# Row-norm Newton steps on VectorE, earlier row loads and re-used buffers for the last gate products in a streaming encoder layer

## Chip, cores, metric

One NeuronCore of a Trainium2 chip runs the whole kernel. The metric is the device time of one execution in microseconds (us). TensorE (PE in the profile) multiplies, VectorE (DVE) and GpSimd (POOL) do elementwise work, ScalarE (ACT) does activations and copies, SyncE (SP) only starts transfers.

## What is computed

One layer of a chunk-causal encoder over 2048 prompt rows and 64 sample rows of width 1024, in float32, with two head groups that share one input product:

```python
h = rms_norm(x, norm_mix_g); z = h @ w_in              # [c_q 384 | c_kv 256 | k_rope 32 | GLU 1024]
q = rms_norm(c_q) @ w_uq;  k, v = expand(rms_norm(c_kv) @ w_ukv, rope(k_r))
attn = softmax(q k^T * scale, chunk-causal) @ v         # 8 heads
u = g[..., :512] * sigmoid(g[..., 512:])                # the gate product
conv = silu(layer_norm(causal_depthwise_conv(u, 31 taps)))
x += concat(rms_norm(attn), rms_norm(conv)) @ w_out
x += square(relu(rms_norm(x) @ w_ff_up)) @ w_ff_down
x += sigmoid(rms_norm(x) @ w_gate) * (p @ w_proj)
y = rms_norm(x, norm_final_g)
```

Every `rms_norm` needs 1/sqrt(mean square) of each row.

## The kernel before

The 17 row tiles (16 of 128 rows and one of 64) form three blocks of two pieces, `T0` and `T1`, of two or three tiles. Each matrix operand is split into a high and a low part, so every product is three matmuls (`mm3`, lines 180 to 182).

**Phase 1** goes through the blocks: latents (`rows`, `latents`, `q_latents`), key and value expansion, queries, and four gate products per piece (`glu(T, j, w)` with j from 0 to 3). A gate product fills two PSUM banks, ScalarE takes the sigmoid of one into a tile `sg` (line 396; two buffers), VectorE multiplies it by the other (397), and SP writes it to memory as `u_s` (398). In the last block PSUM leaves only two banks for these products, so the next one can't begin before line 396 has read the last. For piece `T1` of the last block two slices of the tile are also transposed by TensorE (`new_conv`, 582). Near the end of blocks 0 and 1 the next block's rows are loaded (`load_h`, 236), normalised (`scaled`, 200) and transposed into `thi` and `tlo` (`operand`, 212 to 215). The tile `h` that takes a row tile has four buffers of 4 KB per partition, given out in turn; `queries` also takes one per piece for its table of cosines and sines. The convolution of earlier pieces (`conv_steps`, 614) runs on VectorE as a background sequence: `pin` lets some of its steps follow given instructions.

**The row norms**: `sumsq` squares and sums on ScalarE (162); `rstd` (145 to 157) takes the sums of up to three tiles (up to three columns), makes v (147) and a first guess by integer arithmetic (148, 150) on VectorE, and then does three Newton steps of four instructions each on GpSimd (153 to 156). Layer norms in `conv_steps` call the same function with `tag` "c"; all others with an empty tag.

**Phase 2** is attention. Its pools are laid over phase 1's memory: the first, `ka`, holds the keys and values of the first of three rotating heads (`k0h`, `k0l`, `v0`) and begins where phase 1's pool `p` begins, whose first tile is `h`. So `k0h` (9.25 KB per partition) covers two of the four buffers of `h` and part of the third, and `k0l` the rest of the third and the fourth. Each loads when what lay there is done with: GpSimd starts two transfers into each (lines 668 and 679) and then those into `v0`. TensorE first takes row maxima of scores (719), then products of queries and keys, then those with the values (763, 764). `issue_after` ties the first 24 steps of the maxima to the sigmoid of the gate product j=2 of the last piece. **Phase 3** is the output product, the feed-forward layer, the gate, and the final norm with the write of y (954 to 956).

The order of the instructions on each engine is made by a planner: it takes what is ready by its own reckoning, earlier lines of the program first. Each engine then runs its queue strictly in that order.

Of the kernel before, what the change touches and what calls it, by code (L numbers as in the profile page):

```python
# [9 lines left out]
F32 = mybir.dt.float32  # L10
# [4 lines left out]
ALU = mybir.AluOpType  # L15
# [4 lines left out]
P = 128  # L20
D = 1024
# [46 lines left out]
class Body:  # L68
# [72 lines left out]
    def rstd(self, ss, n, d, eps, tag=""):  # L141
        nc = self.nc
        v = self.sp.tile([P, 4], F32, name=tag + "rv")
        y = self.sp.tile([P, 4], F32, name=tag + "ry")
        t = self.sp.tile([P, 4], F32, name=tag + "rt")
        v, y, t = v[:, :n], y[:, :n], t[:, :n]
        nc.vector.tensor_scalar(out=v, in0=ss, scalar1=1.0 / d, scalar2=eps, op0=ALU.mult, op1=ALU.add)
        nc.vector.tensor_scalar(out=t.bitcast(I32), in0=v.bitcast(I32), scalar1=1, scalar2=None,
                                op0=ALU.logical_shift_right)
        nc.vector.tensor_scalar(out=y.bitcast(I32), in0=t.bitcast(I32), scalar1=-1, scalar2=0x5F3759DF,  # L150
                                op0=ALU.mult, op1=ALU.add)
        for _ in range(3):
            nc.gpsimd.tensor_tensor(out=t, in0=y, in1=y, op=ALU.mult)  # L153
            nc.gpsimd.tensor_tensor(out=t, in0=t, in1=v, op=ALU.mult)
            nc.gpsimd.tensor_scalar(out=t, in0=t, scalar1=-0.5, scalar2=1.5, op0=ALU.mult, op1=ALU.add)
            nc.gpsimd.tensor_tensor(out=y, in0=y, in1=t, op=ALU.mult)  # L156
        return y

    def sumsq(self, out, x, w):
# [63 lines left out]
    def phase1(self):  # L223
        nc, tc, I, O = self.nc, self.tc, self.I, self.O
        self.banks((0, 1, 2, 7), (4, 5, 6), 3)
        with ExitStack() as c:
            p = c.enter_context(tc.tile_pool(name="p1", bufs=2))
            pw = c.enter_context(tc.tile_pool(name="p1w", bufs=2))

            nw = 7  # L230
            def load_h(piece):
                hs = []
                for t in piece.tiles:
                    r0, n = TILES[t]
                    h = p.tile([P, D], F32, name="h", bufs=4)
                    nc.sync.dma_start(out=h[:n, :], in_=I["x"][r0:r0 + n, :])
                    hs.append(h)
                return hs

            def early_t(piece, hs, i):  # L240

                T = make_t(piece, hs)
                y = self.sp.tile([P, 4], F32, name="y0", bufs=2)
                nc.gpsimd.tensor_copy(out=y[:, :3], in_=self.norms(hs, piece.tiles))
                d = self.vp.tile([P, 30 + 384], F32, name="cu", bufs=2)
                for j in range(3):
                    nc.vector.tensor_scalar(out=d[:, j * P:(j + 1) * P], in0=self.ident, scalar1=y[:, j:j + 1],
                                            scalar2=None, op0=ALU.mult)
                tr = self.tr()
                nc.tensor.matmul(tr[:, :384], wide[0][:, 384:], d[:, :384], start=True, stop=True)  # L250
                nc.scalar.copy(out=wide[i][:, :384], in_=tr[:, :384])
                return (*T, y, wide[i][:, :384])
# [7 lines left out]
            def weights(parts, k, c):  # L260

                out = []
                step = WC // c
                for a in range(0, k, step):
                    b = min(k, a + step)
                    x = []
                    raw = pw.tile([P, WC], F32, name="raw")
                    hi = pw.tile([P, WC], F32R, name="whi", bufs=nw)
                    lo = pw.tile([P, WC], F32R, name="wlo", bufs=nw)
                    r, hi, lo = (x[:, :(b - a) * c].rearrange("p (k c) -> p k c", c=c) for x in (raw, hi, lo))  # L270
                    nc.sync.dma_start(out=r, in_=parts[:, a:b, :])
                    self.split(r, hi, lo)
                    out += [(hi[:, i, :], lo[:, i, :]) for i in range(b - a)]
                return out
# [102 lines left out]

                return make

            def glu(T, j, w, n=3):  # L380

                piece, th, tl = T[:3]
                pi = self.pieces.index(piece)
                N = piece.n
                pa, pb = self.mm(), self.mm()
                for ps, c in ((pb, slice(P, 2 * P)), (pa, slice(0, P))):
                    for k in range(KD):
                        self.mm3(ps[:, :N], w[k][0][:, c], w[k][1][:, c], th[:, k, :N], tl[:, k, :N],
                                 k == 0, k == KD - 1)
                u = pw.tile([P, 384], F32, name="sg")  # L390
                if len(T) > 3:
                    nc.vector.tensor_tensor(out=u, in0=pb[:, :N], in1=T[4], op=ALU.mult)
                    nc.scalar.activation(out=u, in_=u, func=AF.Sigmoid)
                    nc.vector.tensor_tensor(out=u, in0=u, in1=T[4], op=ALU.mult)
                else:
                    self.sig[piece, j] = nc.scalar.activation(out=u[:, :N], in_=pb[:, :N], func=AF.Sigmoid)
                r = nc.vector.tensor_tensor(out=u[:, :N], in0=pa[:, :N], in1=u[:, :N], op=ALU.mult)
                nc.sync.dma_start(out=self.u_s[pi][j], in_=u[:, :N])
                if pi == len(self.pieces) - 1:
                    self.new_conv(pw, u, j)  # L400
                self.pin(r, n)

            hs = load_h(self.pieces[0])
# [5 lines left out]
            T0 = early_t(self.pieces[0], hs, 0)  # L409
# [4 lines left out]
            hs = load_h(self.pieces[1])  # L414
            T1 = early_t(self.pieces[1], hs, 1)
            for bi, block in enumerate(self.blocks):
                kv0, cols0 = latents(T0, wkv)
                cq0 = q_latents(T0, wcq)
                kv1, cols1 = latents(T1, wkv)
                if bi == 0:  # L420
                    cq1 = q_latents(T1, wcq)
                wukv = weights(I["wukv"], 2, 1024)
                if bi == 0:
                    past = self.past_keys(p)
                    g0 = weights(I["wglu"][0], KD, 256)
                    q0 = queries(T0, cq0)
                    self.expand_k(p, *past, wukv)
                    glu(T0, 0, g0)
                    self.expand_v(p, *past, wukv)
                    k0 = keys(T0, kv0)  # L430
                    wuq = weights(I["wuq"], 3, 768)
                    glu(T1, 0, g0)
                else:
                    k0 = keys(T0, kv0)
                    q0 = queries(T0, cq0)
                    cq1 = q_latents(T1, wcq)
                    wuq = weights(I["wuq"], 3, 768)
                    g0 = weights(I["wglu"][0], KD, 256)
                self.expand(p, cols0, *k0, wukv)
                k1 = keys(T1, kv1)  # L440
                q0(wuq)
                q1 = queries(T1, cq1)
                if bi:
                    glu(T0, 0, g0)
                self.expand(p, cols1, *k1, wukv)
                g1 = weights(I["wglu"][1], KD, 256)
                q1(wuq)
                if bi:
                    glu(T1, 0, g0)
                g2 = weights(I["wglu"][2], KD, 256)  # L450
                if bi == 2:
                    self.banks((0, 1), (4, 5, 6), 3)
                glu(T0, 1, g1)
                if bi == 0:
                    self.bg = chain(self.conv_steps(0), self.conv_steps(1))
                g3 = weights(I["wglu"][3], KD, 256)
                glu(T1, 1, g1)
                if bi < 2:
                    n0, n1 = self.blocks[bi + 1]
                    wkv = weights(I["wkv"], KD, KVL + ROPE)  # L460
                    hs = load_h(n0)
                    self.scaled(hs, n0, hs)
                glu(T0, 2, g2)
                glu(T0, 3, g3)
                if bi < 2:
                    T0 = make_t(n0, hs)
                    hs = load_h(n1)
                    self.scaled(hs, n1, hs)
                glu(T1, 2, g2, 1)
                glu(T1, 3, g3, 1)  # L470
                if bi < 2:
                    wcq = weights(I["wcq"], KD, QL)
                    T1 = make_t(n1, hs)
# [772 lines left out]
```

## Time and profile before

| what | value |
|---|---|
| median of 3 runs | 3009.92 us (3006.69 to 3010.46) |
| the profiled execution | 3011.01 us, its span 3009.2 us |
| TensorE busy | 2912.3 us, 97% of the span |
| VectorE / ScalarE / GpSimd busy | 65% / 41% / 26% |
| mean granted TensorE clock | 0.990 of full speed |

The span runs from the first to the last instruction; the profiled execution's time is 1.8 us longer. An engine's idle time counts only where TensorE, or the end of the kernel, waits for it.

### The profile page before, as it was taken

The page shows a single profiled execution, that of the slowest core. Times are in us where ns is not written, and L with a number is a line of the kernel's source. Part 1 is how long each engine was busy: PE and PEld are TensorE (multiplying, and loading weights), DVE is VectorE, ACT ScalarE, POOL GpSimd, SP SyncE. Part 2 cuts the span into 40 slices and gives each one's busy share as a digit, 9 for nine tenths or more (in the row PEclk, how much of TensorE's full clock was granted, in tenths as well). Part 3 has the DMA queues.
Part 4 walks back from the last instruction along what each step waited for, and adds up shares of the span by engine and source line. Part 5 has one row for each costly group of instructions (what it writes and reads, how often), then busy time and mean ns, then how long its engine had stood idle before and what let it go on. Part 6 is the DMA issues. An engine that isn't in the chain of part 4 may idle for free.

```text
span 3009.2 us, 42569 instructions
## 1 busy us (share of the span) xinstructions
PE 2912.3 (97%) x15666; PEld 2568.8 (85%) x15666; DVE 1957.0 (65%) x3592; ACT 1242.5 (41%) x2388; POOL 782.1 (26%) x1526
## 2 busy tenths in 40 slices
PE   8998998899999899999999999999999999999998
PEld 7998898677777689999998889988988799999986
DVE  4489694888888756776665457868865544444463
ACT  6334343778878742223224343223234422221242
POOL 3021523878887610003002120012022200000001
PEclk9999999999999999999999999999999999999999
DMA  6636258633231221222112241222223412211131
GB/s 203 208 101 206 84 182 162 104 73 57 59 57 42 83 97 45 80 79 76 61 59 84 85 168 63 98 65 84 97 79 95 140 49 81 88 57 57 64 94 46
DMA packets 148601, 279.13 MB, mean 93 GB/s; under 512 B 38136, under 2 KB 78824, under 8 KB 146952
## 3 DMA queue, kind: packets, MB, share of 16 engines
q1 hardware_dynamic: 123800, 244.35, 25.5%
q0 software_dynamic: 24592, 32.06, 5.6%
q8 instruction: 123, 2.02, 0.3%
q14 instruction: 86, 0.70, 0.1%
HBM read 225.67 MB, written 51.28 MB: 92 GB/s over the span
## 4 chain that ended last, share of the span: by engine, by line
PE 78%; DVE 9%; POOL 4%; issue 4%; DMA 3%; ACT 2%; SPq 0%; DVEq 0%; ACTq 0%; POOLq 0%
PE mm L180 24%; PE mm L181 23%; PE mm L182 23%; PE tr L212 2%; PE low L764 2%; PE acc L763 2%; DVE mx L720 2%; DVE cacc L614 1%; DVE pl L756 1%; PE tr L719 1%; DMA u_s<-sg 1%; DVE ql L706 1%; POOL rt L153 1%; ACT ph L754 1%; POOL ry L156 0%
## 5 line engine op out<-in xcount | busy, mean ns | idle before, releaser
L181 PE MATMUL mm<-tlo,uh 128*128 128x384 f32 (+2 forms) x1488 | 481.4, 324 | 0.0
L180 PE MATMUL mm<-thi,uh 128*128 128x384 f32 (+2 forms) x1488 | 481.1, 324 | 0.0
L182 PE MATMUL mm<-thi,ul 128*128 128x384 f32 (+2 forms) x1488 | 480.9, 323 | 0.0
L614 DVE SCALAR_TENSOR_TENSOR cacc<-cu,cw,cacc 128x384 f32<-128x384 f32 (+2 forms) x720 | 414.3, 590 | 6.7
L1005 ACT ACTIVATE rl<-mm 128x384 f32<-128x384 f32 (+1 forms) x192 | 88.3, 460 | 644.9 <-PE mm L182 644.4
L180 PE MATMUL mm<-wdh,ah 128*128 128x512 f32 x896 | 349.2, 391 | 2.2 <-DVE x L1082 1.7
L181 PE MATMUL mm<-wdl,ah 128*128 128x512 f32 x896 | 348.4, 390 | 0.0
L182 PE MATMUL mm<-wdh,al 128*128 128x512 f32 x896 | 345.0, 390 | 0.0
L760 POOL TENSOR_TENSOR rs<-rs,ph 128x512 f32<-128x512 f32 (+5 forms) x304 | 326.4, 1077 | 40.3 <-ACT ph L754 25.9
L1082 DVE SCALAR_TENSOR_TENSOR x<-mm,y,x 128x512 f32<-128x512 f32 x224 | 166.3, 748 | 212.0 <-PE mm L182 210.1
L153 POOL TENSOR_TENSOR rt<-ry 128x3 f32<-128x3 f32 (+2 forms) x150 | 40.3, 269 | 987.3 <-DVE ry L150 979.4
L181 PEld LDWEIGHTS mm<-tlo,uh 128*128 128x128 f32 x1488 | 280.2, 188 | 0.6
L180 PEld LDWEIGHTS mm<-thi,uh 128*128 128x128 f32 x1488 | 279.9, 188 | 0.7
L182 PEld LDWEIGHTS mm<-thi,ul 128*128 128x128 f32 x1488 | 280.1, 188 | 0.1
L166 DVE TENSOR_TENSOR wdl<-raw,wdh 128x1024 fp32r<-128x1024 f32 x139 | 170.5, 1228 | 112.1 <-ACT wdh L165 110.9
L756 DVE TENSOR_TENSOR pl<-mm,ph 128x512 fp32r<-128x512 f32 (+5 forms) x344 | 193.9, 575 | 43.3 <-ACT mm L755 30.2
L754 ACT ACTIVATE ph<-mm 128x512 fp32r<-128x512 f32 (+5 forms) x344 | 175.9, 511 | 86.8 <-PE mm L182 59.0
L165 ACT CAST wdh<-raw 128x1024 fp32r<-128x1024 f32 x139 | 145.8, 1050 | 158.6 <-DMA raw<-in_wdn 91.8
L180 PEld LDWEIGHTS mm<-wdh,ah 128*128 128x128 f32 x896 | 168.3, 188 | 37.6 <-DVE x L1082 2.2
L182 PEld LDWEIGHTS mm<-wdh,al 128*128 128x128 f32 x896 | 168.2, 188 | 35.0
L181 PEld LDWEIGHTS mm<-wdl,ah 128*128 128x128 f32 x896 | 168.3, 188 | 33.8
L166 DVE TENSOR_TENSOR ul<-raw,uh 128x1024 fp32r<-128x1024 f32 x104 | 128.7, 1237 | 99.7 <-ACT uh L165 98.9
(309 smaller groups left out, 6682.5 us busy)
## 6 DMA issues: line engine op xcount, KB each, us to landing
raw<-in_wup SPq DMA_DIRECT2D x96, 512.0 KB, 3.3
raw<-in_wdn SPq DMA_DIRECT2D x96, 512.0 KB, 3.3
raw<-in_wglu SPq DMA_DIRECT2D x24, 512.0 KB, 4.7
raw<-in_wout SPq DMA_DIRECT2D x24, 512.0 KB, 4.7
raw<-in_wgate SPq DMA_DIRECT2D x24, 512.0 KB, 3.9
v_s<-vst SPq DMA_DIRECT2D x36, 256.0 KB, 2.8
v<-v_s POOLq DMA_DIRECT2D x8, 1152.0 KB, 7.9
h<-in_x SPq DMA_DIRECT2D x16, 512.0 KB, 4.4
```

The costliest lines, as they stand in the source:

```text
L153: nc.gpsimd.tensor_tensor(out=t, in0=y, in1=y, op=ALU.mult)
L165: self.nc.scalar.copy(out=hi, in_=raw)
L166: return (eng or self.nc.vector).tensor_tensor(out=lo, in0=raw, in1=hi.bitcast(F32), op=ALU.subtract)
L180: t.matmul(ps, sh, mh, start=start, stop=False)
L181: t.matmul(ps, sh, ml, start=False, stop=False)
L182: t.matmul(ps, sl, mh, start=False, stop=stop)
L614: nc.vector.scalar_tensor_tensor(out=a, in0=U[:, k:k + W], scalar=w, in1=a, op0=ALU.mult, op1=ALU.add)
L754: nc.scalar.activation(out=ph[b:, s], in_=ps[b:, s], func=AF.Exp)
L756: nc.vector.tensor_tensor(out=pl[b:, s], in0=ps[b:, s], in1=ph[b:, s].bitcast(F32), op=ALU.subtract)
L760: nc.gpsimd.tensor_tensor(out=rs[b:, s], in0=rs[b:, s], in1=ph[b:, s].bitcast(F32), op=ALU.add)
L1005: nc.scalar.activation(out=rl[:, :N], in_=ps[:, :N], func=AF.Relu)
L1082: r = nc.vector.scalar_tensor_tensor(out=x1[t][:n, cs], in0=ps[:n, :], scalar=Y[q][:n, j:j + 1], in1=x1[t][:n, cs], op0=ALU.mult, op1=ALU.add)
```

## The change

Three edits. In `rstd`, calls without a tag do each Newton step with three instructions on VectorE instead of four on GpSimd; calls with tag "c" stay. In blocks 0 and 1 the loads of the next block's first piece stand two gate products (and two weight loads) earlier in the program; their normalisation stays where it was. In the last block the gate products j=2 and j=3 of both pieces write into tiles `h` instead of `sg`.

```diff
         for _ in range(3):
-            nc.gpsimd.tensor_tensor(out=t, in0=y, in1=y, op=ALU.mult)
-            nc.gpsimd.tensor_tensor(out=t, in0=t, in1=v, op=ALU.mult)
-            nc.gpsimd.tensor_scalar(out=t, in0=t, scalar1=-0.5, scalar2=1.5, op0=ALU.mult, op1=ALU.add)
-            nc.gpsimd.tensor_tensor(out=y, in0=y, in1=t, op=ALU.mult)
+            if tag:
...
+            else:
+                nc.vector.scalar_tensor_tensor(out=t, in0=y, scalar=-0.5, in1=y, op0=ALU.mult, op1=ALU.mult)
+                nc.vector.tensor_tensor(out=t, in0=t, in1=v, op=ALU.mult)
+                nc.vector.scalar_tensor_tensor(out=y, in0=t, scalar=1.5, in1=y, op0=ALU.add, op1=ALU.mult)
...
-            def glu(T, j, w, n=3):
+            def glu(T, j, w, n=3, last=False):
...
-                u = pw.tile([P, 384], F32, name="sg")
+                u = p.tile([P, D], F32, name="h", bufs=4)[:, :384] if last else pw.tile([P, 384], F32, name="sg")
...
                 if bi:
                     glu(T1, 0, g0)
+                if bi < 2:
+                    n0, n1 = self.blocks[bi + 1]
+                    hs = load_h(n0)
                 g2 = weights(I["wglu"][2], KD, 256)
...
                 glu(T1, 1, g1)
                 if bi < 2:
-                    n0, n1 = self.blocks[bi + 1]
                     wkv = weights(I["wkv"], KD, KVL + ROPE)
-                    hs = load_h(n0)
                     self.scaled(hs, n0, hs)
-                glu(T0, 2, g2)
-                glu(T0, 3, g3)
+                glu(T0, 2, g2, last=bi == 2)
+                glu(T0, 3, g3, last=bi == 2)
...
-                glu(T1, 2, g2, 1)
-                glu(T1, 3, g3, 1)
+                glu(T1, 2, g2, 1, bi == 2)
+                glu(T1, 3, g3, 1, bi == 2)
```

## Rows read from the trace of the kernel before

**Rows 1.** The page's part 1: busy us, share of the span, instructions.
```profile
PE 2912.3 (97%) x15666; PEld 2568.8 (85%) x15666; DVE 1957.0 (65%) x3592; ACT 1242.5 (41%) x2388; POOL 782.1 (26%) x1526
```

**Rows 2.** Windows: length; busy us of PE, PEld, DVE, ACT, POOL; clock; DMA.
```profile
225.00:300.00 75.00, 65.36 (x404) 62.18 (x404) 68.52 (x138) 32.19 (x67) 14.26 (x43) 0.95 0.64 204
...
352.00:367.00 15.00, 8.52 (x42) 7.05 (x43) 11.52 (x17) 4.88 (x12) 12.09 (x30) 0.81 0.12 44
361.50:374.00 12.50, 9.93 (x37) 8.22 (x38) 11.99 (x23) 3.85 (x9) 4.43 (x7) 0.50 0.12 45
...
471.50:477.00 5.50, 5.50 (x18) 5.31 (x19) 0.96 (x2) 0.59 (x1) 0.00 (x0) 0.50 1.83 297
507.00:515.00 8.00, 4.31 (x14) 2.62 (x15) 5.89 (x24) 3.26 (x6) 4.32 (x9) 0.78 0.67 164
```

**Rows 3.** Waits of PE from 467 to 476 us: total, times, longest.
```profile
PE mm L180 <- ACT sg L396: 4.3, 1, 4.3
```

**Rows 4.** VectorE's timeline at the end: start, duration, instruction [idle before, releaser].
```profile
3000.21 0.15 DVE L148 TENSOR_SCALAR rt<-rv 128x1 int32<-128x1 int32 x1
3000.40 0.15 DVE L150 TENSOR_SCALAR ry<-rt 128x1 int32<-128x1 int32 x1
3003.87 1.28 DVE L954 SCALAR_TENSOR_TENSOR x<-x,ry,gfin 64x1024 f32<-64x1024 f32 x1 [3.32 <-POOL ry L156]
```

**Rows 5.** Tile ry: duration ns minimum/median/maximum, first and last start, forms.
```profile
L153 POOL TENSOR_TENSOR rt<-ry x150: 184/195/2161, 9.5 to 3002.8; 128x3 f32<-128x3 f32 x117, 128x2 f32<-128x2 f32 x24, 128x1 f32<-128x1 f32 x9
...
L150 DVE TENSOR_SCALAR ry<-rt x50: 148/169/1145, 9.3 to 3000.4; 128x3 int32<-128x3 int32 x39, 128x2 int32<-128x2 int32 x8, 128x1 int32<-128x1 int32 x3
```

**Rows 6.** VectorE's timeline in block 1 and at its end.
```profile
262.95 0.55 DVE L570 TENSOR_TENSOR q<-cq,h 128x384 f32<-128x384 f32 x1
...
273.66 0.16 DVE L150 TENSOR_SCALAR ry<-rt 128x3 int32<-128x3 int32 x1
273.73 0.74 DVE L535 TENSOR_TENSOR ktl<-mm,kth 128x256 fp32r<-128x256 f32 x2
...
351.60 2.07 DVE L200 TENSOR_SCALAR h<-h,ry 128x1024 f32<-128x1024 f32 x3 [2.70 <-POOL ry L156]
...
359.79 3.31 DVE L306 SCALAR_TENSOR_TENSOR kv<-kv,ry,gkv 128x256 f32<-128x256 f32 x3 [3.48 <-POOL ry L156]
```

**Rows 7.** GpSimd's timeline between blocks 1 and 2.
```profile
354.21 2.16 POOL L153 TENSOR_TENSOR rt<-ry 128x3 f32<-128x3 f32 x1
...
358.82 0.22 POOL L638 TENSOR_SCALAR nb<-nb 128x1 f32<-128x1 f32 x1
```

**Rows 8.** ScalarE's timeline, at two waits of phase 1.
```profile
359.08 0.81 ACT L639 ACTIVATE cs<-cs,nb,cry 128x512 f32<-128x512 f32 x1 [10.32 <-POOL nb L638]
...
470.85 0.44 ACT L396 ACTIVATE sg<-mm 128x320 f32<-128x320 f32 x1 [8.88 <-DMA u_s<-sg]
```

**Rows 9.** GpSimd's timeline: transfers into the first key tile.
```profile
453.86 0.57 POOL L668 DMA_DIRECT2D k0h<-kr_sh  x1 [42.10 <-DMA q_s<-cq]
...
455.07 0.53 POOL L679 DMA_DIRECT2D k0h<-k_s0h  x1
```

**Rows 10.** SP's timeline: a row load of block 2, and the last gate tile's write.
```profile
263.52 0.34 SPq L236 DMA_DIRECT2D h<-in_x  x1
...
507.24 0.34 SPq L398 DMA_DIRECT2D u_s<-sg  x1
```

**Rows 11.** Tile u_s, 497 to 512 us: writes of gate tiles, issue to landing.
```profile
DMA to landing us min/median/max: 2.1/2.1/2.2
```

**Rows 12.** Tile k0h, 450 to 520 us: its two transfers, issue to landing.
```profile
DMA to landing us min/median/max: 6.9/9.2/11.5
```

**Rows 13.** TensorE's timeline: first maxima and first score product of phase 2.
```profile
506.52 0.28 PE L719 MATMUL tr<-k0h,qh 128*128 128x256 f32 x1
...
515.01 0.63 PE L180 MATMUL mm<-qh,k0h 128*128 128x512 f32 x1
```

**Rows 14.** VectorE's timeline late in phase 2.
```profile
1003.37 1.02 DVE L147 TENSOR_SCALAR rv<-ss 128x3 f32<-128x3 f32 x1 [0.90 <-ACT junk L162]
```

More of the change, by code (lines that the diff above doesn't have):

```diff
@@ L152, in rstd @@
         for _ in range(3):
-            nc.gpsimd.tensor_tensor(out=t, in0=y, in1=y, op=ALU.mult)
-            nc.gpsimd.tensor_tensor(out=t, in0=t, in1=v, op=ALU.mult)
-            nc.gpsimd.tensor_scalar(out=t, in0=t, scalar1=-0.5, scalar2=1.5, op0=ALU.mult, op1=ALU.add)
-            nc.gpsimd.tensor_tensor(out=y, in0=y, in1=t, op=ALU.mult)
+            if tag:
+                nc.gpsimd.tensor_tensor(out=t, in0=y, in1=y, op=ALU.mult)
+                nc.gpsimd.tensor_tensor(out=t, in0=t, in1=v, op=ALU.mult)
+                nc.gpsimd.tensor_scalar(out=t, in0=t, scalar1=-0.5, scalar2=1.5, op0=ALU.mult, op1=ALU.add)
+                nc.gpsimd.tensor_tensor(out=y, in0=y, in1=t, op=ALU.mult)
+            else:
+                nc.vector.scalar_tensor_tensor(out=t, in0=y, scalar=-0.5, in1=y, op0=ALU.mult, op1=ALU.mult)
+                nc.vector.tensor_tensor(out=t, in0=t, in1=v, op=ALU.mult)
+                nc.vector.scalar_tensor_tensor(out=y, in0=t, scalar=1.5, in1=y, op0=ALU.add, op1=ALU.mult)
         return y
```

## The prediction, made before the change was run

> **What bounds the kernel now.** I read the page's busy line first, then windows, then the timelines around each hole of TensorE. TensorE is busy for 2912.3 of 3009.2 us [rows 1], so the change can only win in the 97 us in which it is idle, in stretches where it runs at half its granted clock, and in the tail behind its last matmul. The reader should see three places. Between blocks 1 and 2 TensorE worked 8.52 of 15 us, and then ran at a granted clock of 0.50 (its 1.2 GHz level) while busy for 9.93 us [rows 2]: 6.5 us idle and about half of 9.93, 5.0 us, lost to the clock. Before the last gate products it waited 4.3 us [rows 3] and ran 5.50 busy us at 0.50 behind it [rows 2], another 2.75. And at the very end VectorE waits 3.32 us for GpSimd [rows 4].
>
> **Newton steps: the cost of one norm.** There are 50 norms without the tag (150 instructions of line 153, three a norm) [rows 5]. Each loses 12 GpSimd instructions (0.195 us by the median of line 153) and gains 9 on VectorE. The trace of before has no such instruction on VectorE; the nearest rows are the small integer ones of lines 148 and 150 beside them: 0.15 to 0.17 us each, started 0.19 us apart where one needs the other [rows 4, 5], and only 0.07 us ahead of an instruction that doesn't need them [rows 6]. So a norm costs VectorE between 9 x 0.07 = 0.6 and 9 x 0.19 = 1.7 us.
>
> **The tail.** Line 150 starts at 3000.40 and line 954 at 3003.87 [rows 4]. With nine steps of 0.19 us behind line 150, line 954 starts at about 3000.40 + 10 x 0.19 = 3002.3: 1.6 us gained. Nothing else runs there, so I take it whole.
>
> **Between blocks 1 and 2.** GpSimd runs the untagged chains mixed with the layer norm's chain. One multiply of three numbers took 2.16 us, and the layer norm's last step (line 638) was done only at 359.0 [rows 7]. ScalarE had stood behind it for 10.32 us [rows 8], with the copies that feed TensorE queued after it; VectorE waited 2.70 and 3.48 us for the two untagged chains [rows 6]. Without the untagged steps GpSimd has only the layer norm left. The full prize is 6.5 + 5.0 = 11.5 us, the least is nothing, if the convolution steps that VectorE mixes in hold the nine steps back as long as GpSimd did. VectorE has idle time to fit them in (the two waits), so I take three quarters: 8.6 us gained.
>
> The Trainium skill, page "SBUF — State Buffer", section "Who interferes with whom", says that a VectorE instruction with two SBUF inputs and a GpSimd instruction that reads SBUF exclude each other for a whole instruction. The 2.16 us multiply agrees: it overlapped VectorE's work. By that rule the Newton steps on VectorE, all with two SBUF inputs, can now be the ones that block; where that would matter is a rival below.
>
> **VectorE's extra load.** In 225 to 300 us VectorE is busy 68.52 of 75 us and TensorE idle almost 10 [rows 2]. Three norms fall there and some four in the like stretch of block 2. Seven norms at 0.6 to 1.7 us are 4 to 12 us of VectorE time. At best the 6.5 us left free in that window hide them (0), at worst all of it delays TensorE (12). VectorE already ends waits there, so I take 3 us lost. Elsewhere (phase 3, the gate products) VectorE has room and TensorE none to give: nothing.
>
> **Row loads moved.** Per block these are two or three transfers on SP's queue, put ahead of the loads of two gate weights, of the next latents' weights and of two writes of gate tiles. But a load can't start before its buffer of `h` is free: the third one of block 2 started at 263.52, right behind the last VectorE instruction that reads the table in that buffer (262.95 plus 0.55) [rows 6, 10]. That reader doesn't move, and the load ran far ahead of its place in the program already. I cost it at 0; with the cover gone, one transfer on the queue ahead of a weight is its issue time of 0.34 us [rows 10], times six. On the other side, earlier loads gain nothing that a held buffer allows.
>
> **Gate tiles in `h`: what it removes.** At 453.86 GpSimd starts loading the first head's keys [rows 9]. These transfers crowd the write of an earlier gate tile: ScalarE stood 8.88 us for it [rows 8], and TensorE 4.3 [rows 3]. But the stalled product is j=1, which the change leaves in `sg`. It is relieved all the same, since the key loads no longer run at that time (next paragraph). Gain: 4.3 + 2.75 = 7.0 us.
>
> **What it adds.** The four tiles take the four buffers of `h` in turn, and the last of them (piece T1, j=3) gets the third buffer, which `k0h` and `k0l` share. Before, the key load waited for the last reader of `h`, at 453 us. Now it waits until the very last gate tile is written out. That write was issued at 507.24 [rows 10], 0.7 us behind the last gate matmul, and lands 2.1 us later [rows 11]; GpSimd can then issue, some 3.0 us behind the last matmul. `k0h` is complete when its second transfer lands: 455.07 + 11.5 - 453.86 = 12.7 us after the first issue [rows 9, 12]. Phase 2's first maxima came at 506.52, at once behind the gate products [rows 13]; now they come 15.7 us behind. TensorE has nothing else to do. Behind the waiting transfers in GpSimd's queue stand those for the second head and the layer norm's steps; they are not due at once. What comes back: in 507 to 515 TensorE was idle for 3.7 us [rows 2], on work of VectorE and ScalarE that can now be done during the wait; I take back 3.0. Cost 12.7 us, between 9 (faster landing without other traffic) and 18 (values late too).
>
> **The sum.** -1.6 - 8.6 + 3 + 0 - 7.0 + 12.7 = -1.5 us against the profiled execution's 3011.0, which is 1.1 above the median. I forecast 3008 us: no change that can be told. About 0.2%, 6 us, is what a measurement of this kernel can tell from none.
>
> **Rivals.**
> 1. Both prizes in full: transition 11.5, VectorE's load hidden (0), start of phase 2 at 11.2: -1.6 - 11.5 - 7.0 + 11.2 = -8.9, so 3001 us. For it: VectorE's waits for GpSimd around 352 to 360. Against: a window with 91% VectorE.
> 2. The change does not tie the keys to the last gate tile (other buffers, or a wait that I misread): without the 12.7 the sum is -14.2, so 2996. Against it: the wait of 42.10 us that ended at the last reader of `h` [rows 9].
> 3. Slower: VectorE becomes the bound of blocks 1 and 2. Newton steps stand in its queue ahead of the low parts that TensorE needs; transition gain 0, load 10: -1.6 + 10 - 7.0 + 12.7 = +14, so 3024. It decides from about 8 us of the seven norms on TensorE's path. Against: VectorE's idle time in the transition.
> 4. Slower: the second head's keys go out ahead of the first head's on GpSimd's queue, since their memory is free when the last gate matmul ends, 3 us sooner. Another 12.7 us or more: 3021 and up, about 3026. Against: first in program order are the first head's.
> 5. Slower, late in phase 2: two norms there run beside GpSimd's long additions. A small VectorE instruction took 1.02 us there [rows 14] against 0.17; 18 of them cost up to 18 x 0.85 = 15 us of VectorE time, and I put 8 on the path: 3016. This is the exclusion rule of the page "SBUF — State Buffer" of the Trainium skill, turned against the change.
>
> **How the numbers follow.** Forecast 0.40 (its own range 3002 to 3014), rivals 1 to 5: 0.20, 0.13, 0.12, 0.09, 0.06. Faster by over 0.2%: rivals 1 and 2 and a little of the forecast's edge, 0.34. Slower: rivals 3, 4 and 5, 0.27. Within: 0.39. The range 2994 to 3025 leaves out most of rival 4 and the lower edge of rival 2, and part of the far values of the transition and the load.
>
> **What would show it.** Tail: nine VectorE instructions and line 954 some 2 us behind line 150. Transition: TensorE's hole at 352 to 367 down to a few us and no stretch at clock 0.50. Gate products: no wait for the write of `u_s`. Start of phase 2: the first transfer into `k0h` directly behind the last write of `u_s`, and a hole of some 15 us in TensorE. The forecast is wrong if that hole is missing or twice as long, or if the holes in blocks 1 and 2 grow together with VectorE's busy share.

## The result, and the profile after

The changed kernel takes 3030.98 us (median of 6 runs, 3028.10 to 3032.66) against 3010.1 for the kernel before: ratio 1.0072, interval 1.0062 to 1.0082. It is slower by 0.7%, some 21 us; the prediction had said 3008 and a range up to 3025. The span of the profiled execution grew from 3009.2 to 3028.8 us, 19.6.

The page's part 1 of the changed kernel (columns as in [rows 1]) shows where the Newton steps went, 55 us more of VectorE and 152 less of GpSimd, and that TensorE, with the same 15666 matmuls, is busy 7.3 us longer:

```profile
PE 2919.6 (96%) x15666; PEld 2575.3 (85%) x15666; DVE 2011.7 (66%) x4042; ACT 1242.5 (41%) x2388; POOL 630.1 (21%) x926
```

To see where the span grew, both traces are cut at the same places of TensorE's work: the start of its 2000th, 2200th and 2600th matmul (by which both kernels have done the same work but for a handful of matmuls), the end of the last gate product, the first maxima, the start of the 3250th and 5500th matmul, and the end of the last one. The windows of the kernel before (columns as in [rows 2]; the hole has no length there):

```profile
0.00:347.08 347.08, 321.92 (x2000) 311.73 (x2001) 232.28 (x463) 157.19 (x320) 93.03 (x300) 0.98 0.53 172
347.08:390.23 43.15, 36.60 (x202) 33.26 (x201) 33.55 (x64) 15.55 (x37) 25.83 (x77) 0.84 0.13 45
390.23:460.81 70.58, 67.96 (x401) 64.16 (x401) 65.60 (x132) 29.81 (x60) 17.62 (x41) 1.00 0.67 207
460.81:506.69 45.88, 41.59 (x251) 40.76 (x249) 12.06 (x28) 9.79 (x22) 17.67 (x40) 0.93 0.67 132
506.69:606.49 99.80, 86.38 (x403) 63.16 (x403) 83.20 (x188) 71.07 (x153) 73.29 (x91) 0.95 0.78 129
606.49:1086.85 480.36, 451.46 (x2252) 339.94 (x2251) 399.64 (x819) 367.76 (x828) 355.93 (x392) 0.99 0.28 65
1086.85:2996.68 1909.83, 1906.39 (x10167) 1715.82 (x10165) 1126.37 (x1896) 590.21 (x967) 194.79 (x570) 1.00 0.24 80
```

and those of the changed kernel:

```profile
0.00:341.54 341.54, 320.49 (x2001) 311.16 (x2001) 244.22 (x571) 156.28 (x319) 44.71 (x136) 0.99 0.54 174
341.54:379.81 38.27, 34.37 (x201) 31.74 (x201) 35.36 (x87) 15.84 (x37) 22.71 (x35) 0.91 0.19 58
379.81:458.87 79.06, 70.14 (x402) 65.54 (x401) 69.53 (x159) 29.62 (x62) 9.71 (x25) 0.98 0.54 175
458.87:497.44 38.57, 38.57 (x250) 38.01 (x248) 10.44 (x25) 7.23 (x17) 15.22 (x39) 1.00 0.14 45
497.44:514.16 16.72, 0.40 (x4) 0.14 (x3) 3.25 (x17) 1.61 (x4) 7.20 (x12) 0.59 0.99 197
514.16:620.18 106.02, 92.02 (x400) 66.45 (x401) 83.01 (x179) 72.55 (x155) 71.65 (x87) 0.89 0.97 138
620.18:1105.24 485.06, 455.99 (x2251) 344.63 (x2250) 403.52 (x854) 368.22 (x827) 346.36 (x344) 0.98 0.28 64
1105.24:3017.25 1912.01, 1907.62 (x10167) 1717.59 (x10165) 1156.75 (x2139) 589.95 (x967) 112.50 (x252) 1.00 0.25 80
```

The lengths, line by line: blocks 0 and 1 (up to the 2000th matmul) -5.5; between blocks 1 and 2 (to the 2200th) -4.9; block 2 up to its last gate products (to the 2600th) +8.5; these gate products -7.3; the hole +16.7; the start of phase 2 +6.2; its rest +4.7; phase 3 +2.2. The tail behind the last matmul went from 12.6 to 11.6 us. Together +19.6. In phase 2 behind the hole nearly all of the growth is busy time of TensorE on the same work (92.02 against 86.38, 455.99 against 451.46), and the granted clock in the same lines is lower: that part is clock, not waiting.

The hole, in TensorE's timeline of the changed kernel (the line that answers to [rows 13]), with SP's and GpSimd's timelines of the same microseconds (to [rows 9, 10]), one fence each:

```profile
498.10 0.39 PE L588 MATMUL tr<-ident,h 128*30 128x128 f32 x2 [0.66 <-DVE h L402]
514.16 1.62 PE L725 MATMUL tr<-k0h,qh 128*128 128x128 f32 x4 [15.67 <-DMA k0h<-k_s0h]
```

```profile
498.07 0.35 SPq L403 DMA_DIRECT2D u_s<-h  x1
```

```profile
500.48 0.53 POOL L674 DMA_DIRECT2D k0h<-kr_sh  x1 [1.51 <-DMA u_s<-h]
...
501.63 0.51 POOL L685 DMA_DIRECT2D k0h<-k_s0h  x1
```

The last gate tile is written out at 498.07; GpSimd had waited for that write and starts the keys at 500.48, 46.6 us later than before; and TensorE stands 15.67 us for the second of them. The prediction's hole is there, a little longer: the first maxima come 16.7 us behind the last gate product (497.44), where 15.7 stood. The 15.67 of the row count from the transposes behind it.

The keys were not alone in being late. The queries' first load (`qr`, SP) went out at 457.63 before and at 499.57 here, and ScalarE's copy of it, from which the maxima read, was done at 510.04. With the keys on time, a hole of some 12.6 us (an estimate: 510.04 - 497.44) would have been left.

Between blocks 1 and 2, VectorE's timeline of the changed kernel shows what became of the Newton steps (lines 159 to 161; it answers to [rows 6]):

```profile
339.97 0.15 DVE L159 SCALAR_TENSOR_TENSOR rt<-ry 128x3 f32<-128x3 f32 x1
340.04 1.18 DVE L620 SCALAR_TENSOR_TENSOR cacc<-cu,cw,cacc 128x384 f32<-128x384 f32 x2
341.14 0.17 DVE L160 TENSOR_TENSOR rt<-rt,rv 128x3 f32<-128x3 f32 x1
...
351.78 0.15 DVE L161 SCALAR_TENSOR_TENSOR ry<-rt,ry 128x3 f32<-128x3 f32 x1
...
352.98 0.75 DVE L205 TENSOR_SCALAR h<-h,ry 128x1024 f32<-128x1024 f32 x1
```

The planner puts one or two steps of a norm, then two steps of the convolution (some 1.14 us), then the next ones. The norm that begins its nine steps at 339.97 has the last at 351.78, and line 205, which scales the rows by it, follows: 12.0 us for nine steps of 0.15. On GpSimd the twelve steps of this norm took 5.6 us; its timeline in the kernel before, first and last step:

```profile
345.94 0.54 POOL L153 TENSOR_TENSOR rt<-ry 128x3 f32<-128x3 f32 x1
...
351.38 0.19 POOL L156 TENSOR_TENSOR ry<-ry,rt 128x3 f32<-128x3 f32 x1
```

The steps begin 6 us sooner, TensorE being 5.5 us ahead by then, and end no sooner. All the same TensorE gains here. Its waits between the 2000th and 2200th matmul (total, times, longest), in the kernel before and then in the changed one:

```profile
PE mm L180 <- ACT thi L214: 3.4, 1, 3.4
PE tr L212 <- DVE tlo L215: 2.6, 1, 2.6
```

```profile
PE tr L217 <- DVE h L205: 3.5, 1, 3.5
```

The waits for the operand's two halves, `thi` and `tlo`, are gone but for 0.4 us, and one for the scaled rows has grown from 0.6: 3.9 us idle where 6.6 were, and a granted clock of 0.91 where it was 0.84. Block 2 then loses more than that: between the 2200th and 2600th matmul TensorE is idle for 8.9 us where 2.6 were. Its longest waits there in the changed kernel:

```profile
PE tr L499 <- POOL kr L580: 3.5, 1, 3.5
PE mm L185 <- DVE ry L161: 2.2, 1, 2.2
```

The second is for the last step of a norm. The first is for the rotation of the keys' position part on GpSimd, whose first product of 16 columns took 0.73 us before and 4.67 after (GpSimd's timelines, a fence each):

```profile
384.68 0.73 POOL L567 TENSOR_TENSOR ra<-kv,cs 128x16 f32<-128x16 f32 x1 [7.31 <-ACT kv L292]
```

```profile
375.72 4.67 POOL L573 TENSOR_TENSOR ra<-kv,cs 128x16 f32<-128x16 f32 x1 [8.39 <-ACT kv L297]
```

A later product of that rotation took 2.73 us and ended at 383.74. VectorE worked without a pause from before 375.72 until 383.76.

Late in phase 2, VectorE's and then GpSimd's timeline of the changed kernel (to [rows 14]), and the wait of TensorE that comes of it:

```profile
1013.15 1.02 DVE L148 TENSOR_SCALAR rt<-rv 128x3 int32<-128x3 int32 x1
...
1015.16 0.88 DVE L159 SCALAR_TENSOR_TENSOR rt<-ry 128x3 f32<-128x3 f32 x1
...
1017.25 1.11 DVE L160 TENSOR_TENSOR rt<-rt,rv 128x3 f32<-128x3 f32 x1
1018.29 0.68 DVE L762 TENSOR_TENSOR pl<-mm,ph 128x512 fp32r<-128x512 f32 x1
```

```profile
1012.85 1.30 POOL L766 TENSOR_TENSOR rs<-rs,ph 128x512 f32<-128x512 f32 x1 [0.31 <-ACT ph L760]
1014.75 1.28 POOL L766 TENSOR_TENSOR rs<-rs,ph 128x512 f32<-128x512 f32 x1 [0.60 <-ACT ph L760]
```

```profile
1019.02 0.45 PE L770 MATMUL low<-pl,v 128*66 128x512 f32 x1 [2.02 <-DVE pl L762]
```

A small step that meets a GpSimd addition lasts until that addition ends: 1013.15 + 1.02 = 1014.17 against 1012.85 + 1.30 = 1014.15, and 1015.16 + 0.88 = 1016.04 against 1014.75 + 1.28 = 1016.03; beside no addition it takes 0.16, and one that began in the same instant as an addition (1017.05) took 0.16 too. The low part at 1018.29 stood behind the last of these, and TensorE 2.02 us behind the low part.

The tail, VectorE's timeline of the changed kernel (to [rows 4]): from line 150 to line 960 it is 1.93 us, 3.47 before.

```profile
3021.51 0.15 DVE L150 TENSOR_SCALAR ry<-rt 128x1 int32<-128x1 int32 x1
...
3023.44 1.28 DVE L960 SCALAR_TENSOR_TENSOR x<-x,ry,gfin 64x1024 f32<-64x1024 f32 x1
```

### The profile page after: what moved, and what is told of

The parts are those of the page before. It is cut to its first block, busy times and chain, and to the rows that moved or that the text cites. A ratio compares the mean times of both kernels' runs of the same rounds, so it can differ in the third digit from the quotient of the medians.

```text
span 3028.8 us, 42441 instructions
## 1 busy us (share of the span) xinstructions
PE 2919.6 (96%) x15666; PEld 2575.3 (85%) x15666; DVE 2011.7 (66%) x4042; ACT 1242.5 (41%) x2388; POOL 630.1 (21%) x926
## 3 DMA queue, kind: packets, MB, share of 16 engines
q8 instruction: 123, 2.02, 0.3%
## 4 chain that ended last, share of the span: by engine, by line
PE 80%; DVE 7%; DMA 5%; ACT 3%; POOL 2%; issue 2%; SPq 0%; DVEq 0%; ACTq 0%; POOLq 0%
PE mm L185 24%; PE mm L186 24%; PE mm L187 24%; PE tr L217 2%; PE acc L769 2%; PE low L770 2%; DVE mx L726 1%; PE tr L725 1%; DVE pl L762 1%; DMA qr<-in_mq 1%; DVE cacc L620 1%; DMA qr<-q_s 1%; DMA raw<-in_wglu 1%; DMA v_s<-vst 1%; DMA h<-in_x 0%
## 5 line engine op out<-in xcount | busy, mean ns | idle before, releaser
L185 PE MATMUL mm<-wdh,thi 128*128 128x512 f32 x454 | 179.1, 398 | 3.7 <-DVE rt L148 3.0
```

The costliest lines, as they stand in the source:

```text
L185: t.matmul(ps, sh, mh, start=start, stop=False)
```

## The experiments

Two theories stood at the start. **Keys**: the loss is the first head's keys, which wait for the last gate tile. **VectorE**: the loss is the Newton steps. The first four kernels take the parts one by one.

**Gate tiles alone** (kernel before, the lines of the diff with `last`):

```diff
-                u = pw.tile([P, 384], F32, name="sg")
+                u = p.tile([P, D], F32, name="h", bufs=4)[:, :384] if last else pw.tile([P, 384], F32, name="sg")
```

> The kernel before with one part of the change: the four gate tiles in the buffers of h. Theory (keys): the cost of the change is that the key loads wait for the last gate tile. Then the hole of 15.7 us ahead of the first maxima is here too, the stall on the gate products (some 6 us with the clock) is gone, and phase 2 starts with late values and late keys of the second head, some 5 us more: about 15 to 17 us above the kernel before, 3026. Rival (VectorE): the cost comes from the Newton steps, and the hole is paid for by what is gained ahead of it: within 8 us of the kernel before, 3010 to 3018.

3022.21 us against 3009.12, ratio 1.0045 (1.0032 to 1.0058). TensorE's wait ahead of the first maxima in this kernel:

```profile
PE tr L719 <- DMA k0h<-k_s0h: 15.2, 1, 15.2
```

Some 13 of the 21 us are this edit's: 2 to 4 less than expected, and more than the rival allows.

**Newton steps alone** (kernel before, the lines of the diff in `rstd`):

```diff
+            if tag:
...
+            else:
+                nc.vector.scalar_tensor_tensor(out=t, in0=y, scalar=-0.5, in1=y, op0=ALU.mult, op1=ALU.mult)
+                nc.vector.tensor_tensor(out=t, in0=t, in1=v, op=ALU.mult)
+                nc.vector.scalar_tensor_tensor(out=y, in0=t, scalar=1.5, in1=y, op0=ALU.add, op1=ALU.mult)
```

> The kernel before with one part of the change: Newton steps of the untagged norms on VectorE. Theory (keys): little is left: 5 us gained in blocks 0 and 1, 1 us at the tail, against some 6 us late in phase 2 and 2.7 us around 2090 us: 3008 to 3014. Rival (VectorE): the steps stand between the convolution steps and make TensorE late at every norm: 3020 or more.

3013.29 us, ratio 1.0014 (1.0005 to 1.0023): a small loss, as the theory of the keys has it. In the trace TensorE is 4.0 us ahead at the first maxima (502.51 against 506.52), and has lost it all by the end of phase 2.

**All but the gate tiles** (changed kernel, without `last`):

```diff
-                glu(T0, 2, g2, last=bi == 2)
-                glu(T0, 3, g3, last=bi == 2)
+                glu(T0, 2, g2)
+                glu(T0, 3, g3)
...
-                glu(T1, 2, g2, 1, bi == 2)
-                glu(T1, 3, g3, 1, bi == 2)
+                glu(T1, 2, g2, 1)
+                glu(T1, 3, g3, 1)
```

> The changed kernel without the gate tiles in h (Newton steps and earlier row loads stay). Theory (keys): the key loads start some 45 us ahead of the first maxima again, no hole there, and the stall on the gate products is back: 3010 to 3015. Rival (VectorE): 3020 or more. If the row loads matter, this differs from the kernel with the Newton steps alone by more than 3 us.

3015.67 us, ratio 1.0022 (1.0012 to 1.0032): just beyond the theory's range and below the rival's. It is 2.4 us above the kernel with the Newton steps alone, less than the 3 us set for the row loads to matter. With the gate tiles' 1.0045 it makes 1.0067, and the whole change 1.0072: the parts about add up.

**Two of the four tiles** (changed kernel; T0's stay in `h`):

```diff
-                glu(T1, 2, g2, 1, bi == 2)
-                glu(T1, 3, g3, 1, bi == 2)
+                glu(T1, 2, g2, 1)
+                glu(T1, 3, g3, 1)
```

> The changed kernel with only the two tiles of piece T0 in h, those of T1 in sg again. Theory (keys): they take the second and the first buffer of h; the first head's high keys wait for the second of them, written out at about 484 us, and land at about 496, just ahead of the first maxima (498); so no hole, and no key loads in the time of the stalled gate product: about 6 us below the changed kernel without gate tiles in h, 3004 to 3009. Rival (VectorE): 3018 or more.

3025.58 us, ratio 1.0053 (1.0041 to 1.0066): the rival's time, but not for its reason. The keys start when expected (GpSimd's timeline, 486.61) and the hole is indeed only 2.7 us, but two other waits took its place (TensorE's waits, 497 to 530 us):

```profile
PE tr L725 <- DVE mw L726: 9.4, 1, 9.4
PE tr L725 <- ACT ncv L590: 5.6, 1, 5.6
...
PE tr L725 <- DMA k0h<-k_s0h: 2.7, 1, 2.7
```

Now the key loads run when the last two gate tiles are written out: the write issued at 490.28 took 12.1 us to land (2.1 in [rows 11]), and SP, with its loads of queries (`qr`) queued around it, issued the last tile's write only at 503.50. The 9.4 us are for maxima whose queries came that late: ScalarE waited 5.47 and 6.97 us for `qr`. I had moved the collision, not removed it. What matters is when the keys load, so I looked for a tile that leaves them where they were.

**Gate tiles in the value tiles' buffers** (kernel before; also j=1 of T1, the product that stalled):

```diff
-                u = pw.tile([P, 384], F32, name="sg")
+                if last:
+                    u = p.tile([P, NH // 2, 2, 64], F32R, name="vst", bufs=3)
+                    u = u.rearrange("p a b c -> p (a b c)").bitcast(F32)[:, :384]
+                else:
+                    u = pw.tile([P, 384], F32, name="sg")
```

> The kernel before; in the last block the gate tile of T1 with j=1 and the four behind it go in turn into the three buffers of the value tiles (vst), which are long free by then and don't lie under the first head's keys. Theory (keys): the loads of the first head's keys start at 454 as before, so no hole ahead of the first maxima; and the sigmoid of j=1, which waited for a write of an earlier tile crowded by these loads, needs no such tile any more: the 4.3 us and the 2.75 us at half clock are gained, 3002 to 3005. Rival (the relief of the gate products needs the key loads out of the way, since later tiles then wait for the same crowded writes): 3007 to 3011.

3024.79 us, ratio 1.0044 (1.0030 to 1.0058): neither case. GpSimd's timeline in this kernel:

```profile
494.54 0.62 POOL L649 DMA_DIRECT2D s_s<-cs  x1 [0.30 <-POOL cs L648]
495.17 0.55 POOL L672 DMA_DIRECT2D k0h<-kr_sh  x1
```

The keys wait for no gate tile here, but they stand behind the layer norm's write in GpSimd's queue: they come 41 us later than before, although by my reckoning their memory is free. They are not what TensorE waited for: they landed at 506.9, and it stood 13.9 us for the queries (`qh`), whose first load went out at 499.95 and which landed only at 511.7. So keys and queries are late together, as in the changed kernel. `vst`, like `h`, belongs to the pool `p` under the first head's keys. I take it that with tiles of that pool in use up to the end of phase 1 the planner puts the loads behind them; the kernel with the weights' buffers below fits that, but does not show it alone.

**Newton steps in phase 1 and at the end only** (kernel before with the steps, but not in `prepare` and `operand`, lines 874 and 939):

```diff
-            if tag:
+            if tag or not vec:
...
-            y = self.norms([h[q] for h in hs], pc.tiles, CC)
+            y = self.norms([h[q] for h in hs], pc.tiles, CC, False)
```

> The kernel before with the Newton steps on VectorE for the norms of phase 1 and of the last line alone; those of the attention's output and of the third phase stay on GpSimd. Theory (shared time late in phase 2): the 3.5 to 6.5 us that the kernels with all steps on VectorE lose between 900 and 1087 us come from those 18 steps a norm beside GpSimd's long additions; without them the 4 us gained by the end of phase 1 are kept, and 1 us at the tail: about 3005. Rival (the loss late in phase 2 is only another order of the same work): as the kernel with all Newton steps on VectorE, 3010 to 3014.

3011.47 us, ratio 1.0005 (0.9996 to 1.0014): no difference from before, and the rival's time. My theory was only partly right; see the windows below.

**That with the value tiles' buffers**: both edits of the last two.

> Both of the last two together. If their gains add up: -6 and -5, 2998 to 3001. If the Newton steps on VectorE take away what the gate products gained (VectorE busier in block 2): 3003 to 3006.

3025.91 us, ratio 1.0057 (1.0045 to 1.0070): the late loads again, and again it is the queries that TensorE waits for ahead of the first maxima (TensorE's timeline). The keys had landed at 512.25.

```profile
515.89 1.72 PE L728 MATMUL tr<-k0h,qh 128*128 128x128 f32 x4 [16.58 <-ACT qh L714]
```

**Gate tiles in the weights' buffers**, which belong to the other pool (kernel before; j=1 of T1, j=2 and 3 of T0):

```diff
-                u = pw.tile([P, 384], F32, name="sg")
+                if last:
+                    u = pw.tile([P, WC], F32R, name="whi", bufs=nw).bitcast(F32)[:, :384]
+                else:
+                    u = pw.tile([P, 384], F32, name="sg")
```

> The kernel before; in the last block the gate tile of T1 with j=1 and the two of T0 with j=2 and 3 go into buffers of the weight tiles (whi), which belong to the other pool of phase 1. Theory (any gate tile in the pool that lies under the first head's keys moves their loads behind it, in memory or in GpSimd's program): here the loads start at 454 as before, no hole; the stalled gate product is gone (4.3 us and 2.75 us at half clock): 3002 to 3006. Rival (every shift ahead of phase 2 is paid back in phase 2 by a lower clock, as in the kernels with Newton steps on VectorE): 3008 to 3012, with more than the 8 us at half clock that phase 2 of the kernel before loses.

3003.64 us, ratio 0.9984 (0.9975 to 0.9993): faster, as the theory has it. GpSimd's timeline and TensorE's waits from 460 to 503 us in this kernel:

```profile
450.42 0.57 POOL L671 DMA_DIRECT2D k0h<-kr_sh  x1 [42.09 <-DVE cacc L617]
```

```profile
PE mm L180 <- ACT whi L399: 1.5, 1, 1.5
```

The keys load early, the queries too (first load at 454.58), there is no hole, and of the stalled gate product's 4.3 us [rows 3] 1.5 are left, with no stretch at half clock behind it (101.33 us from the 2250th matmul to the end of the gate products, 107.63 before).

**The changed kernel with these tiles**: the same edit, in the place of `h`.

> The changed kernel with the gate tiles in buffers of whi (T1 j=1, T0 j=2 and 3) in place of those of h; Newton steps and row loads as changed. Theory (keys): the hole of 15.7 us and the 6 us behind it go, the relief of the gate products stays: some 20 us below the changed kernel, 3009 to 3012. Rival: the hole was only in part the tiles' doing: 3016 or more.

3011.03 us, ratio 1.0005 (0.9996 to 1.0014): 20 us below the changed kernel, by the choice of buffers. (It also leaves the last two tiles of T1 in `sg` and takes j=1 in; the place and the choice of the tiles are not separated.)

**Row loads alone**:

```diff
+                if bi < 2:
+                    n0, n1 = self.blocks[bi + 1]
+                    hs = load_h(n0)
...
-                    n0, n1 = self.blocks[bi + 1]
-                    hs = load_h(n0)
```

> The kernel before with one part of the change: the next block's row loads two gate products earlier in the program. By the prediction's step a held buffer lets nothing start earlier: within 2 us of the kernel before, and the same times up to the start of phase 2. Rival: the loads stand ahead of weights on SP's queue and cost up to 2 us, or they release the norms earlier and gain up to 5.

3009.65 us, ratio 1.0001 (0.9992 to 1.0010): nothing, as costed.

**The fastest version**: gate tiles in the weights' buffers, Newton steps on VectorE in the last norm only.

```diff
-                y = self.norms([x1[t] for t in tiles], tiles)
+                y = self.norms([x1[t] for t in tiles], tiles, vec=True)
```

> The kernel before with gate tiles in whi as above, and the Newton steps on VectorE for the last norm alone. If the gains add up: 1.0 to 1.6 us below the kernel with gate tiles in whi, about 3002 to 3005, the fastest version. If the order of phase 2 costs the gain again: 3007 to 3011.

3001.82 us against 3009.15, ratio 0.9981 (0.9972 to 0.9990). It beats the kernel before and the changed one; against the one without the last norm's edit the 1.8 us lie inside the intervals, but its tail is 11.6 us where that one's is 12.6.

**Late Newton steps on top of that** (`prepare`, line 874, with `vec` true):

> The kernel with gate tiles in whi and the last norm's Newton steps on VectorE; now the steps of the attention output's norms (late in phase 2) on VectorE too. Theory (steps beside GpSimd's long additions): each takes up to 1 us there, some of it ahead of a low part that TensorE needs: late phase 2 is 3 to 6 us longer than in the kernel without this edit, 3005 to 3008. Rival (only the other order of phase 2, which comes from the steps in phase 1, costs time): within 1.5 us of it, 3000 to 3003.

3004.36 us, ratio 0.9990 (0.9981 to 0.9998). The windows from the 3250th to the 5500th matmul, for the kernel with those of phase 1 and the end, the fastest version, and this one, a fence each:

```profile
605.48:1089.15 483.67, 454.67 (x2251) 342.74 (x2250) 398.37 (x817) 368.17 (x827) 357.55 (x393) 0.98 0.28 64
```

```profile
600.93:1079.51 478.58, 449.78 (x2252) 338.86 (x2251) 400.56 (x819) 367.58 (x828) 355.03 (x392) 1.00 0.28 65
```

```profile
599.69:1081.62 481.93, 452.52 (x2251) 340.95 (x2250) 405.10 (x855) 368.20 (x828) 345.73 (x344) 0.99 0.27 64
```

The late steps cost 481.93 - 478.58 = 3.35 us there. The steps of phase 1, with the late ones left on GpSimd, cost 483.67 - 480.36 = 3.3 in the same window, though none of them runs in it. All steps together (Newton steps alone, 486.39) cost 6.0. These are single executions: the six kernels with the steps of phase 1 and the late ones on GpSimd lie between 478.3 and 480.4, the three with steps of phase 1 but not the late ones on VectorE at 483.7 to 485.0, the five with both at 485.1 to 487.1. So both parts stand clear of that spread, but the 3.35 could be 1.6 to 3.6. Theory and rival each hold in part; that the order is what costs the rest is not shown (below).

**Newton steps of the row tiles on top of the fastest** (`scaled`, with `vec` true):

> The kernel with gate tiles in whi and the last norm's Newton steps on VectorE; now the steps of the row tiles' norms in phase 1 (not those of latents and queries) on VectorE too. If these norms are what the transition between blocks 0 and 1 gained by, TensorE is 3 to 5 us earlier at its matmul 1500, and if phase 2 keeps it, 2997 to 3000. Rival (phase 2 comes out in another order and loses it): 3002 to 3007.

3017.95 us, ratio 1.0029 (1.0017 to 1.0042), worse than even the rival. TensorE is 6.6 us ahead of the fastest version at its 1500th matmul (268.82 against 275.40): these norms are what blocks 0 and 1 gained by. Then it waits at the start of phase 2 (its waits, 497 to 560 us) for a layer norm's copy, which itself waits for the norm's last write, issued at 502.78 among the key loads and landed at 515.96:

```profile
PE tr L727 <- ACT cs L638: 11.8, 1, 11.8
```

The median lies 4.4 to 7.7 us above the profiled span in four kernels (Newton steps alone, all but the gate tiles, two of the four tiles, and this one), and 0.6 to 2.5 in the others; what the windows say holds for the profiled executions.

## Why the prediction was wrong

**Start of phase 2.** The mechanism was right: the keys' first transfer starts 3.0 us behind the last gate product, as worked out, and the second one landed 12.4 us after its issue (11.5 before), which makes 16.7 us of hole where 15.7 stood; that the row of the wait says 15.67 is chance. (The row of the 42.10 us wait names the write of the queries, `q_s`, and no reader of `h`; the wait for the write of `u_s` at 500.48 bears the reading out all the same.) The step that failed is the sentence "I take back 3.0" with its bound "between 9 ... and 18" for the whole cost. In the first 8 us behind the hole TensorE was idle for 1.5 us where [rows 2] has 3.7, so some 2 us came back, but at a granted clock of 0.57:

```profile
514.16:522.16 8.00, 6.46 (x23) 4.97 (x23) 4.18 (x10) 3.78 (x6) 1.77 (x2) 0.57 2.22 247
```

Over the first 100 us nothing was left of it: 14.0 us idle against 13.4 (2.1 of them a wait for the values, which the bound had named), and 5.6 us more of busy time at a lower clock. The prediction had priced the half clock behind the two holes of before, and put it at nothing behind the one that it forecast itself. The hole cost 16.7 and the 100 us behind it 6.2, which is 22.9 where 12.7 stood: half of the miss. It also had the keys alone in view, and the queries were late too. That the tiles cause it is shown by the kernels without them in `h` (20 us with the weights' buffers). Rival 4, the nearest in time, is not what happened: the second head's keys went out at 504.50, behind the first head's.

**Between blocks 1 and 2.** I took three quarters of 11.5, 8.6, as gained, and 4.9 came. ScalarE's wait for the layer norm fell from 10.3 to 3.8 us, and with it TensorE's for the copies, as forecast. The rest stayed for the reason given with the least case: convolution steps between the Newton steps, 3.5 us of TensorE's time.

**VectorE's extra load** was put at +3; blocks 0 and 1 gained 5.5, and block 2 lost 8.5. That this makes +2.9 is luck, two errors that cancel. In blocks 0 and 1 I had looked at the added instructions only. TensorE's wait for the low part of the keys, `ktl`, between 225 and 300 us before (total, times, longest) went from 6.5 to 3.2 us at its longest:

```profile
PE mm L180 <- DVE ktl L535: 7.4, 2, 6.5
```

With the row tiles' norms alone on VectorE its longest is 1.6 us; there the planner has put that low part ahead of weight splits that stood before it in VectorE's queue. In block 2 the loss is rival 3's, 8.5 of its 10 us, but for the rotation on GpSimd and a norm's last step rather than for low parts. Both effects go with the steps of phase 1: the seven kernels that have all of them on VectorE took 37.9 to 39.3 us from the 2000th to the 2200th matmul and 77.8 to 80.9 from there to the 2600th; the seven without took 42.3 to 43.3 and 69.8 to 70.6. With the row tiles' norms alone it is 42.1 and 77.9: most of the loss, and little of the gain.

**Gate tiles' relief**: 7.0 predicted, 7.3 measured (45.88 to 38.57 us), and as much in the kernel with gate tiles alone (38.53). Right, with the reason given: no wait for a crowded write, and no half clock behind it.

**Rest of phase 2 and phase 3** stood in the sum at nothing, and cost 4.7 and 2.2. (The 2.2 may be spread: phase 3 takes 1911.74 us, 1.9 more than before, in the kernel with gate tiles in the weights' buffers, which changes nothing there.) Rival 5 (8 us) described the late steps; alone they cost some 3.35. By the Trainium skill, page "SBUF — State Buffer", section "Who interferes with whom", the first of two such instructions holds the shared ports and the other blocks until it is done, and a VectorE instruction with one input can be caught as well where it runs in a two-port mode; the trace agrees in the ends that fall together, line 148 (one input, 1.02 us) among them, though no trace here shows in which mode that one ran. The other half comes with the steps of phase 1, and no step of mine held it.

**Tail**: 1.0 of 1.6. VectorE needed 1.93 us from line 150 to the scaling, as forecast, but the rest of the tail moved by half a microsecond. **Row loads**: 0, right.

With the forecast's -1.5: +10.2 (start of phase 2), +3.7 (transition), -0.1 (VectorE's load), -0.3 (gate products), +4.7, +2.2 and +0.6 (tail) make +19.5 by these windows.

**What stays open**: why phase 2 runs at a lower clock when only phase 1's norms changed. Compared record by record, TensorE's order in phase 2 is that of the kernel before in the fastest version, with row loads alone and with gate tiles in the weights' buffers, and another in the eight kernels that have Newton steps of phase 1 on VectorE. But the kernels with gate tiles alone and with those in the value tiles' buffers have another order too, and their late windows are 479.83 and 479.87 us, no longer than before. So another order alone does not bring the loss, and it is not shown to be its cause.

## What to carry to other kernels

Where a tile is borrowed from a pool, look at what is laid over that pool next: a buffer that is free now may be the start signal of the next phase's loads, in memory or in the planner's order, and 20 us hung on that choice here. Small steps moved to an engine with a background sequence come out spread through it: what waits for them waits for the chain's length in the queue (12 us for nine steps of 0.15), not for their sum. Cut the trace where the terms of the sum end: here a gain of 4.9 us and a loss of 8.5 lie next to each other, and a window over both shows neither. And a gain ahead of a phase boundary is only kept if what the next phase starts with is early too.

## What the runs showed of the hardware

TensorE's granted clock made up most of what phase 2 lost behind the hole: between the first maxima and its 5500th matmul it was busy 548.0 us in the changed kernel and 537.8 before, on the same work, idle for about the same time. And a VectorE instruction of 0.16 us that meets a GpSimd addition of 1.3 us ended with it, the one with a single input too. The other way round, a GpSimd product of 16 columns took 4.67 us instead of 0.73 beside VectorE's work without a pause.
